# A count read ahead of the gather, overflow pieces nested in each other, and a last expert done by halves of its inner features

## The chip, the cores and the metric

The kernel runs on one core of a Trainium2 chip. The core has a matrix engine (TensorE, PE in the rows; its weight loads stand as PEld), three engines for elementwise work (VectorE or DVE, ScalarE or ACT, GpSimd or POOL), a queue engine that only issues transfers here (SyncE, SP), and 16 DMA engines that move data between the off-chip memory (HBM) and the on-chip memory (SBUF). Matrix results land in eight accumulator banks (PSUM). The metric is the device time of one execution in microseconds (us), less is better.

## What is computed

One encoder block: a token mixer (attention and a state-space scan, not touched here), then a mixture of experts over 256 tokens of 1024 features, with 32 experts of 1024 inner features, of which each token takes four.

```python
logits = xt @ w_router + b_router
top_val, top_idx = lax.top_k(logits, TOP_K)
top_w = jax.nn.softmax(top_val, axis=-1)
combine = jnp.sum(jax.nn.one_hot(top_idx, N_EXPERTS, dtype=xt.dtype) * top_w[..., None], axis=1)
for e in range(N_EXPERTS):
    gu = xt @ w_gate_up[e] + b_gate_up[e]
    gate = jnp.minimum(gu[:, :EXPERT_FF], SWIGLU_LIMIT)
    up = jnp.clip(gu[:, EXPERT_FF:], -SWIGLU_LIMIT, SWIGLU_LIMIT)
    act = (up + 1.0) * gate * jax.nn.sigmoid(SWIGLU_ALPHA * gate)
    out = out + combine[:, e:e + 1] * (act @ w_down[e] + b_down[e])
...
res = res + gate_f * _rmsnorm(ffn, p(g_post_ffn))
```

All of it is float32. The weights of one expert are 8 MiB for gate and up and 4 MiB for down.

## The kernel before

**Weights.** All weight tiles pass through one ring of SBUF slots of 1 MiB (`consumed`, L134). A load is issued on SP when a slot is released, which is when PE has read the tile that was in it. Each load also waits for the eighth load before it to have landed, since there are eight completion semaphores in turn. An expert has 12 loads: eight tiles of `w_gate_up` (128 of the 1024 input features by all 2048 columns, in rows of 8 KiB) and four of `w_down` (256 inner features by 1024 columns, in pieces of 4 KiB). The last expert's four `w_down` tiles are cut another way: 512 inner features by 512 columns, in pieces of 2 KiB, so that one half of the output columns can be finished before the other.

**Start of the experts (L995 to L1048).** Matmuls with a triangle of ones give each token its rank in each expert's list (`rank`) and each expert's count of tokens (`cnt`). `keep_warm` issues matmuls whose result nobody reads. `select` makes a 0/1 matrix for two experts, and `gather` multiplies it with the token rows, so that `xg` holds up to C = 64 tokens for each of the two experts.

**The loop (L1211 on).** The body for expert e is written out 32 times, engine by engine, in this order: `more(e, n)`, the rest of an expert with more than 64 tokens; `count(e + 1)`, which reads the next expert's count into a register of PE, ACT and DVE; `gate_up`, 64 tokens by 2048 columns, the two halves of the columns side by side in the array; `glu`; `scatter` of the expert before; half a `gather` for a later pair; `turn`, which transposes; `hint(e + 1, n)`, which tells the sequencers which way the next branch goes; `sel_T`; `down`. `down` leaves `py`, which is copied to `y` at the start of the next round.

**Overflow.** `more` is a branch over four pieces of code, for tokens 64 to 95, 96 to 159, 160 to 223 and 224 to 255. The first stands straight behind the branch. Each other piece has a branch of its own, one behind the other, so that an expert with 65 to 96 tokens comes past three further branches that all skip their piece. A piece reads all 12 tiles of its expert, and none is released until the main part that follows has read them. The profiled data have one such expert, number 11.

**Ahead of the loop** stand four matmuls with a zero tile that clear the four output banks `oacc` (L1206), then `count(0)` and `hint(0, n)`, then the branch of `more(0, n)`.

**The last expert** leaves the loop behind `glu` and `scatter`. Then come `sel_T`, `turn`, and for each half `c` of the output columns: `down` for that half alone, a copy to `y`, a `scatter` of that half, and the part of the final norm that can be done (`final`).

Of the kernel before, what the change touches and what calls it, by code (L numbers as in the profile page):

```python
# [9 lines left out]
F32 = mybir.dt.float32  # L10
# [8 lines left out]
P = 128  # L19
# [15 lines left out]
WARM = (11, 4, 4, 5)  # L35
# [39 lines left out]
def tile_hybrid_block(  # L75
# [42 lines left out]
    for e in range(NE):  # L118
        for k in range(KD):
            add_k(w_gate_up[0, e], k, 1, 0, 2 * FF)  # L120
# [10 lines left out]
    def consumed(n):  # L131
# [3 lines left out]
        while free and ring["next"] < len(loads):  # L135
# [3 lines left out]
            t3, s3, nk = t.rearrange("p (k n) -> p k n", k=shape[1]), src.rearrange("(k p) n -> p k n", p=P), shape[1]  # L139
            step = nk // 2 if i + 1 == len(loads) else nk  # L140
            for k in range(0, nk, step):
                sp.dma_start(t3[:, k:k + step], s3[:, k:k + step])
# [28 lines left out]
    ident_b = pers.tile([P, P], BF16, name="ident_b")  # L171
    wr = pers.tile([P, KD, NE], F32, name="wr")
# [7 lines left out]
    dve.memset(ones_b, 1.0)  # L180

# [816 lines left out]
    idle = pq("u", 1)  # L998
# [34 lines left out]
    sel_n = select((0, 1), 0, C)  # L1033
    for ks in HALF:
        gather(sel_n, xgs[0], ks)
# [13 lines left out]

    oacc = [[mq.tile([P, 512], F32, name=f"o{t}{hf}", tag=f"o{2 * t + hf}") for hf in range(2)] for t in range(2)]  # L1050
# [30 lines left out]
    def from_ring(e):  # L1081
        def get(k, o, w):
            i, k2 = W_MOE + 12 * e + k, k - KD
            if k >= KD and e + 1 < NE:
                i, o = W_MOE + 12 * e + KD + k2 // 2, 1024 * (k2 % 2) + o
            elif k >= KD:
                i, o = W_MOE + 12 * e + KD + 2 * (o // 512) + k2 // 4, 512 * (k2 % 4) + o % 512
            return wt[i][:, o:o + w]
# [75 lines left out]

    def more(e, n):
# [28 lines left out]
    engines = [ET.PE, ET.Activation, ET.DVE]  # L1194

    def count(e):
        return nc.values_load(cnt[0:1, e:e + 1], engines=engines, min_val=0, max_val=S)

    def hint(e, n):
        tc.mark_branch_hint_location(f"more{e}", hint=(n > C), engines=engines)  # L1200

    zero_b = mo.tile([3 * NE, P], BF16, name="zero_b")
    dve.memset(zero_b, 0.0)
    for t in range(2):
        for hf in range(2):
            pe.matmul(oacc[t][hf], zero_b, bias3[:, 0:512], start=True, stop=False, skip_group_check=True)  # L1206

    n = count(0)
    hint(0, n)
    py = None  # L1210
    for e in range(NE):  # L1211
# [3 lines left out]
        if e + 1 < NE:  # L1215
            n = count(e + 1)
# [14 lines left out]
        if e + 1 == NE:  # L1231
            break
# [21 lines left out]

    spare = [free.pop(0).tile([P, SLOT], F32, name=f"spare{i}", tag="w") for i in range(2)]
    jk = spare[1][:, 0:512]
    fo = [[spare[0][:, 1024 * t + 512 * i:1024 * t + 512 * i + 512] for i in range(2)] for t in range(2)]

    rsf = []

    def final(t, hf):
        if t is None:
            for i in range(2 * hf):
                dve.tensor_mul(fo[i][0], oacc[i][0], gbf[0])
            return
        act.activation(jk, oacc[t][hf], AF.Square, accum_out=tiny[:, 4 + 2 * t + hf:5 + 2 * t + hf])
        if hf == 0:
            return
        rsf.append(norm_of(4, t))
        if t == 0:  # L1270
            dve.tensor_mul(fo[0][1], oacc[0][1], gbf[1])
        else:
            act.activation(fo[0][1], fo[0][1], AF.Copy, scale=rsf[0])
            for t, i in ((0, 0), (0, 1), (1, 0), (1, 1)):
# [50 lines left out]
```

## Time and profile before

| | |
|---|---|
| median of three runs | 1322.29 us (1318.12 to 1325.5) |
| the profiled execution's own time | 1321.95 us |
| its span from first to last instruction | 1320.2 us |
| mean granted TensorE clock | 0.978 of 2.4 GHz |
| busy share of the span | PE 89%, DVE 27%, ACT 21%, POOL 2% |
| moved to and from HBM | 466.01 MB, mean 353 GB/s |

The busy shares are averages over stages with different limits: the token mixer up to about 320 us, the start of the experts, the expert loop from 345 us, and the end from about 1290 us. A row of the view by windows gives, for one stretch, its length, each engine's busy time with the number of instructions, the granted clock as a share of full speed (0.50 is 1.2 GHz, 1.00 is 2.4 GHz), the mean busy share of the 16 DMA engines (just over 1.00 where they are full), and what they moved. In the timeline a row has start, duration, engine, line, operation and operands, and in brackets how long the engine sat idle before it and what ended that.

### The profile page before, as it was taken

What the parts mean: (1) busy time and instruction counts of PE and PEld (TensorE: products, weight loads), DVE (VectorE), ACT (ScalarE), POOL (GpSimd) and SP (SyncE); (2) the same over time, 40 slices, a digit from 0 to 9 for tenths busy, and PEclk for the clock granted to TensorE, in tenths of its full rate; (3) what the DMA queues carried; (4) which work ended last, traced back from release to release, by engine and by line L of the source; (5) the groups of instructions that cost most, each with busy time, mean ns of one, the idle gap of its engine ahead of it and who ended that gap; (6) DMA issues with size and microseconds to landing.
All of it is one profiled execution on the core that took longest, in us unless ns stands there. A gap on an engine that the chain in (4) does not pass through costs nothing. (4 is left out here: it accounts for less than half of the span.)

```text
span 1320.2 us, 17110 instructions
## 1 busy us (share of the span) xinstructions
PE 1172.1 (89%) x6842; PEld 580.0 (44%) x6842; DVE 360.5 (27%) x763; ACT 279.1 (21%) x617; POOL 24.9 (2%) x35
## 2 busy tenths in 40 slices
PE   3799989988799999989949999999999999998986
PEld 1788867766333333333423333333333433333322
DVE  0685664457121111211111111211112111111113
ACT  1576556643110000110110001100001011000001
POOL 0100100000000000000000000000000000000000
PEclk9899999999799999999989999999999999999999
DMA  8877745477599999999988999999999999999992
GB/s 313 255 246 249 229 156 192 174 296 292 233 417 412 415 414 415 414 414 413 415 345 317 413 413 413 414 412 414 417 414 409 415 416 414 412 415 411 409 387 94
DMA packets 113469, 466.01 MB, mean 353 GB/s; under 512 B 10955, under 2 KB 34163, under 8 KB 79507
## 3 DMA queue, kind: packets, MB, share of 16 engines
q1 hardware_dynamic: 112576, 462.39, 88.6%
q8 instruction: 109, 1.79, 0.6%
q10 hardware_dynamic: 723, 1.33, 0.3%
q14 instruction: 61, 0.50, 0.1%
HBM read 462.65 MB, written 1.05 MB: 351 GB/s over the span
## 5 line engine op out<-in xcount | busy, mean ns | idle before, releaser
L1104 PE MATMUL pq_g<-w,xg 128*64 128x512 f32 x1024 | 270.9, 601 | 4.1 <-DMA w<-in_w_gate_up_dram 3.1
L1104 PE MATMUL pq_u<-w,xg 128*64 128x512 f32 x1024 | 269.2, 598 | 2.3 <-issue 2.3
L1142 PE MATMUL pq_u<-w,aT 128*64 128x512 f32 x1008 | 226.8, 595 | 2.2
L1116 ACT ACTIVATE sg<-g 128x512 f32<-128x512 f32 (+1 forms) x33 | 20.6, 623 | 730.8 <-DVE g L1115 708.8
L1115 DVE TENSOR_SCALAR g<-pq_g 128x512 f32<-128x512 f32 (+1 forms) x33 | 22.6, 684 | 481.9 <-PE pq_g L1104 266.1
L1104 PEld LDWEIGHTS pq_u<-w,xg 128*64 128x64 f32 x1024 | 75.7, 138 | 144.9 <-issue 142.8
L1104 PEld LDWEIGHTS pq_g<-w,xg 128*64 128x64 f32 x1024 | 75.1, 138 | 139.0 <-issue 117.4
L1142 PEld LDWEIGHTS pq_u<-w,aT 128*64 128x64 f32 x1008 | 70.6, 137 | 136.7 <-issue 124.7
L376 PE MATMUL ps_pj<-hh,wh 128*128 128x256 f32 x296 | 89.6, 303 | 3.6 <-DVE hh L434 3.6
L368 DVE TENSOR_TENSOR wl<-w,wh 128x1024 fp32r<-128x1024 f32 x60 | 74.7, 1246 | 59.0 <-ACT wh L367 58.9
L376 PE MATMUL ps_pj<-hh,wl 128*128 128x256 f32 x296 | 85.6, 289 | 2.4 <-DVE wl L368 2.4
L376 PE MATMUL ps_pj<-hl,wh 128*128 128x256 f32 x296 | 85.5, 289 | 0.0
L1214 DVE COPY y<-pq_u 128x512 f32<-128x512 f32 x31 | 21.4, 692 | 228.4 <-PE pq_u L1142 227.5
L1025 PEld LDWEIGHTS pq_m<-sel,xt 128*128 128x128 f32 x544 | 64.8, 195 | 24.0 <-issue 23.2
L1025 PE MATMUL pq_m<-sel,xt 128*128 128x128 f32 (+1 forms) x544 | 70.9, 285 | 0.0
L1028 ACT ACTIVATE xg<-pq_m,modT,g 128x128 f32<-128x128 f32 x128 | 48.1, 456 | 106.5 <-PE pq_m L1025 106.5
L367 ACT ACTIVATE wh<-w 128x1024 fp32r<-128x1024 f32 x60 | 63.5, 1058 | 29.0 <-PE ps_t L376 10.8
L1153 PE MATMUL o<-y,sT 64*128 64x512 f32 x256 | 65.6, 615 | 1.6 <-DVE y L1290 1.6
L376 PEld LDWEIGHTS ps_pj<-hh,wh 128*128 128x128 f32 x296 | 58.3, 197 | 9.5 <-issue 9.0
L376 PEld LDWEIGHTS ps_pj<-hh,wl 128*128 128x128 f32 x296 | 57.9, 196 | 2.9 <-DVE wl L368 2.8
L376 PEld LDWEIGHTS ps_pj<-hl,wh 128*128 128x128 f32 x296 | 58.0, 196 | 0.1
L1100 PE MATMUL pq_g<-bias,kb 96*64 96x512 bf16 (+1 forms) x68 | 13.7, 406 | 46.0 <-DVE y L1214 26.4
(301 smaller groups left out, 1001.8 us busy)
## 6 DMA issues: line engine op xcount, KB each, us to landing
w<-in_w_gate_up_dram SPq DMA_DIRECT2D x256, 1024.0 KB, 19.0
w<-in_w_down_dram SPq DMA_DIRECT2D x127, 1024.0 KB, 20.0
w<-in_w_ada_dram SPq DMA_DIRECT2D x24, 1024.0 KB, 5.2
w<-in_w_in_dram SPq DMA_DIRECT2D x22, 1024.0 KB, 13.0
w<-in_w_out_dram SPq DMA_DIRECT2D x8, 1024.0 KB, 4.8
xt<-in_x_dram ACTq DMA_DIRECT2D x1, 1024.0 KB
w<-in_w_down_dram SPq DMA_DIRECT2D x2, 512.0 KB
out_dram<-xt SPq DMA_DIRECT2D x4, 256.0 KB, 2.2
```

Source lines behind the costliest of these rows:

```text
L367: act.activation(hi.bitcast(F32R), src, AF.Copy)
L368: dve.tensor_sub(lo.bitcast(F32R), src, hi)
L376: pe.matmul(out_ap, u, v, start=first and i == 0, stop=last and i == 2, skip_group_check=True)
L1025: pe.matmul(p[:, w * i:w * i + w], res[:, t, k * 128:(k + 1) * 128], sel[:, t], start=(t == 0), stop=(t == 1))
L1028: act.activation(xg[:, k], p[:, w * i:w * i + w], AF.Identity, bias=m_shift[:, k:k + 1], scale=g1[:, 8 + k:9 + k])
L1100: pe.matmul(dst[cs * q:cs * q + cs, 0:w], kbv["e3"][0:3 * NE, e:e + 1].to_broadcast([3 * NE, cs]), bias3[:, o:o + w], start=True, stop=Fal ...
L1104: pe.matmul(dst[cs * q:cs * q + cs, 0:w], xg[:, k], weight(k, o, w), start=False, stop=(k == KD - 1), tile_position=(0, cs * q), skip_grou ...
L1115: dve.tensor_scalar(g, pg, 7.0, None, op0=OP.min)
L1116: act.activation(s, g, AF.Sigmoid, scale=1.702)
L1142: pe.matmul(py[cs * q:cs * q + cs, 0:w], a4[:, k % nj, k // nj, :], weight(KD + k, w * q, w), start=(k == 0), stop=(k == KD - 1), tile_pos ...
L1153: pe.matmul(oacc[t][hf], sT[64 * q:64 * q + 64, 128 * t:128 * t + 128], y[64 * q:64 * q + 64, :], start=False, stop=False, tile_position=( ...
L1214: dve.tensor_copy(y, py)
```

## The change

Three edits, one at each end of the loop and one inside `more`.

1. `count(0)` and `hint(0, n)` stand ahead of the first `gather`. The matmuls that clear `oacc` take the place of the nine `keep_warm` matmuls between the rank matmuls, two and two (`clear`); the zero tile is written at the kernel's start.
2. The overflow pieces are nested: the branch for a later piece stands inside the piece before it, with a hint ahead of that piece, and its skipped side leads past all later pieces at once.
3. The last expert's `w_gate_up` is loaded by halves of its inner features: four tiles hold gate and up columns of features 0 to 511 for all input features, four those of 512 to 1023, each as two transfers of 512 KiB in pieces of 2 KiB. Its `w_down` is cut as for the other experts, in pieces of 4 KiB. The computation goes by the same halves: `gate_up_half(0)`, `glu_half(0)`, the scatter before, `gate_up_half(1)` with the first half's transposes inside, `glu_half(1)`, and `down_piece` for both halves of the output columns at once. One final norm follows, on DVE and ACT alone.

```diff
@@ weight loads
+            if e + 1 < NE:
+                add_k(w_gate_up[0, e], k, 1, 0, 2 * FF)
+            else:
+                f = 512 * (k // 4)
+                loads.append(([P, 2, 2, 512], w_gate_up[0, e, 256 * (k % 4):256 * (k % 4) + 256].rearrange(
+                    "p (g n) -> p g n", g=2)[:, :, f:f + 512]))
...
-            if e + 1 < NE:
-                add_k(w_down[0, e], 2 * i, 2, 0, D)
-            else:
-                add_k(w_down[0, e], 4 * (i % 2), 4, 512 * (i // 2), 512)
+            add_k(w_down[0, e], 2 * i, 2, 0, D)
@@ start of the experts
+    def clear(t):
+        for hf in range(2):
+            pe.matmul(oacc[t][hf], zero_b[:, 0:1].to_broadcast([3 * NE, P]), bias3[:, 0:512], start=True, stop=False, skip_group_check=True)
...
-    keep_warm(idle, WARM[2])
+    clear(0)
...
-    keep_warm(idle, WARM[3])
+    clear(1)
...
     sel_n = select((0, 1), 0, C)
...
+    n = count(0)
+    hint(0, n)
     for ks in HALF:
         gather(sel_n, xgs[0], ks)
@@ overflow
+    def rest(e, n, i, chunk):
+        last = i + 1 == len(MORE)
+        if not last:
+            lo = MORE[i + 1][0]
+            tc.mark_branch_hint_location(f"more{e}_{i}", hint=(n > lo), engines=engines)
+        chunk(*MORE[i])
+        if not last:
+            with tc.If(n > lo, preferred_fallthrough_block=True, label=f"more{e}_{i}"):
+                rest(e, n, i + 1, chunk)
...
         with tc.If(n > C, preferred_fallthrough_block=True, label=f"more{e}"):
-            chunk(*MORE[0])
-            for lo, cs in MORE[1:]:
-                with tc.If(n > lo):
-                    chunk(lo, cs)
...
+            rest(e, n, 0, chunk)
@@ last expert
+    gate_up_half(0, range(KD))
+    glu_half(0)
+    scatter(C, y, sTs[(e - 1) % 2])
+    gate_up_half(1, range(4))
+    turn_half(0)
+    gate_up_half(1, range(4, KD))
+    glu_half(1)
+    py = pq("m", 2)
+    down_piece(0, (0, 1))
+    turn_half(1)
+    down_piece(0, (2, 3))
+    down_piece(1, range(4))
...
+    dve.tensor_copy(y[0:C], py[0:C])
+    act.activation(y2[C:P], py[C:P], AF.Copy)
...
+    for t in range(2):
+        for hf, y_ in enumerate((y, y2)):
+            pe.matmul(oacc[t][hf], sT[C * hf:C * hf + C, 128 * t:128 * t + 128], y_[C * hf:C * hf + C, :],
+                      start=False, stop=True, tile_position=(C * hf, 0), skip_group_check=True)
+        for hf in range(2):
+            act.activation(jk, oacc[t][hf], AF.Square, accum_out=tiny[:, 4 + 2 * t + hf:5 + 2 * t + hf])
+            dve.tensor_mul(fo[t][1 - hf], oacc[t][1 - hf], gbf[1 - hf])
+        rsf.append(norm_of(4, t))
+    for t in range(2):
+        for hf, sl in enumerate(halves):
+            dve.scalar_tensor_tensor(res[:, t, sl], fo[t][hf], rsf[t], res[:, t, sl], op0=OP.mult, op1=OP.add)
+            sp.dma_start(out_rows[128 * t:128 * t + 128, sl], res[:, t, sl])
-    for c in range(2):
-        py, rs_ = pq("gu"[c], 1), slice(64 * c, 64 * c + 64)
-        down(e, a4, C, py, (c,))
-        dve.tensor_copy(y[rs_], py[rs_])
-        final(None, c)
-        scatter(C, y, sTs[e % 2], (c,), lambda t: final(t, c))
```

On PE, at the start of the experts, the order before was this, from the first gather (L1025) over the clearing of the output banks (L1206) to the read of the first count (L1197 and L1200); the hint (L1320) and the branch of `more(0, n)` (L1188) follow directly.

```order
L1025 MATMUL pq_m<-sel,xt 128x128 x16
L1206 LDWEIGHTS zero_b
L1206 MATMUL o_3509<-bias_82,zero_b 128x512
L1206 LDWEIGHTS zero_b
L1206 MATMUL o_3510<-bias_82,zero_b 128x512
L1206 LDWEIGHTS zero_b
L1206 MATMUL o_3511<-bias_82,zero_b 128x512
L1206 LDWEIGHTS zero_b
L1206 MATMUL o_3512<-bias_82,zero_b 128x512
L1197 TENSOR_LOAD cnt
L1197 ISA x2
L1200 REGISTER_ALU
```

And this is PE's order there in the changed kernel, from the second pair of clearing matmuls (L1012) to the branch (L1223).

```order
L1012 LDWEIGHTS zero_b
L1012 MATMUL o_3452<-bias_82,zero_b 128x512
L1012 LDWEIGHTS zero_b
L1012 MATMUL o_3453<-bias_82,zero_b 128x512
L1052 TENSOR_LOAD cnt
L1052 ISA x2
L1055 REGISTER_ALU
L1381 BRANCH_PREFETCH_HINT
L1040 MATMUL pq_m<-sel,xt 128x128 x16
L1223 COMPARE_AND_BRANCH
```

The clearing and the read of the count have moved ahead of the gather's 16 matmuls, and the branch now stands straight behind the gather.

On PE, inside the overflow code of one expert before, a piece ends with its scatter (L1153) and the jumps that close it; then comes the next piece's branch, and then that piece's gather (L1025).

```order
L1153 MATMUL o_3512<-ym,sT_3513 128x512
L1191 UNCONDITIONAL_BRANCH x2
L1191 COMPARE_AND_BRANCH
L1025 MATMUL pq_m<-sel,xt 128x64 x16
L1100 LDWEIGHTS kb
```

The same place in the changed kernel:

```order
L1177 MATMUL o_3453<-ym,sT_3530 128x512
L1197 COMPARE_AND_BRANCH
L1194 REGISTER_ALU
L1381 BRANCH_PREFETCH_HINT
L1040 MATMUL pq_m<-sel,xt 128x64 x16
L1124 LDWEIGHTS kb
```

No jump closes a piece before the next branch any more; each piece begins with the hint for the branch at its own end, about 500 PE instructions later.

On SP, the last expert's loads before, from the last two of its eight tiles of `w_gate_up`:

```order
L142 DMA w_25581<-in_w_gate_up_dram 128x2048
L142 DMA w_25587<-in_w_gate_up_dram 128x2048
L142 DMA w_26203<-in_w_down_dram 128x4x512
L142 DMA w_26209<-in_w_down_dram 128x4x512
L142 DMA w_26215<-in_w_down_dram 128x4x512
L142 DMA w_26221<-in_w_down_dram 128x2x512 x2
```

And in the changed kernel:

```order
L145 DMA w_26387<-in_w_gate_up_dram 128x2x512 x2
L145 DMA w_26394<-in_w_gate_up_dram 128x2x512 x2
L150 DMA w_27038<-in_w_down_dram 128x2x1024
L150 DMA w_27044<-in_w_down_dram 128x2x1024
L150 DMA w_27050<-in_w_down_dram 128x2x1024
L150 DMA w_27056<-in_w_down_dram 128x1024 x2
```

The pieces of 512 columns (2 KiB) have moved from the four tiles of `w_down` to the eight of `w_gate_up`, and each of those eight is two transfers.

## Rows read from the trace of the kernel before

**Rows 1.** The page's DMA share in 40 slices of 33 us, and GB/s.

```profile
DMA  8877745477599999999988999999999999999992
GB/s 313 255 246 249 229 156 192 174 296 292 233 417 412 415 414 415 414 414 413 415 345 317 413 413 413 414 412 414 417 414 409 415 416 414 412 415 411 409 387 94
```

**Rows 2.** View by windows: the start, the steady loop, the stall, the last loads.

```profile
core 0: us, PE busy (x) PEld busy (x) DVE busy (x) ACT busy (x) POOL busy (x), PEclk, DMA share, GB/s
336.00:352.00 16.00, 8.56 (x24) 2.57 (x26) 2.07 (x13) 2.84 (x6) 0.00 (x0) 0.57 0.16 51
400.00:640.00 240.00, 223.53 (x1102) 85.79 (x1100) 40.31 (x85) 22.32 (x56) 0.00 (x0) 1.00 1.02 414
682.00:702.00 20.00, 7.86 (x28) 2.66 (x30) 0.00 (x0) 0.00 (x0) 0.00 (x0) 0.57 0.40 150
684.00:690.00 6.00, 0.00 (x0) 0.00 (x0) 0.00 (x0) 0.00 (x0) 0.00 (x0) 0.50 0.63 244
1280.00:1284.00 4.00, 2.91 (x16) 0.57 (x14) 0.00 (x0) 0.00 (x0) 0.00 (x0) 1.00 0.70 272
1284.00:1290.00 6.00, 5.39 (x24) 1.58 (x24) 2.10 (x4) 0.63 (x1) 0.00 (x0) 1.00 1.01 361
```

**Rows 3.** Line L1188, the branch of `more`, 369 to 600 us: duration in ns.

```profile
L1188 PEldq COMPARE_BRANCH  x9: 2960/3257/3452, 369.5 to 596.0; - x9
```

**Rows 4.** Timeline of the start: PE, and SP's first issue after it.

```profile
331.47 4.02 PE L1025 MATMUL pq_m<-sel,xt 128*128 128x128 f32 x32
338.87 1.89 PE L1206 MATMUL o<-bias,zero_b 96*128 96x512 bf16 x4 [3.38 <-DVE zero_b L1203]
345.33 0.64 PE L1100 MATMUL pq_g<-bias,kb 96*64 96x512 bf16 x2 [4.57 <-PEq L1188]
349.84 4.56 SPq L142 DMA_DIRECT2D w<-in_w_down_dram  x3
```

**Rows 5.** Lines L1188 and L1197 at the start, PE's sequencer: duration in ns, start.

```profile
L1188 PEldq COMPARE_BRANCH  x1: 3872/3872/3872, 340.5 to 340.5; - x1
L1197 PEldq TENSOR_LOAD <-cnt x1: 492/492/492, 339.4 to 339.4; - x1
```

**Rows 6.** Lines L1188 and timeline of PE about one branch of the steady loop.

```profile
L1188 PEldq COMPARE_BRANCH  x1: 3283/3283/3283, 397.7 to 397.7; - x1
395.50 6.61 PE L1142 MATMUL pq_u<-w,aT 128*64 128x512 f32 x30
403.00 0.41 PE L1100 MATMUL pq_g<-bias,kb 96*64 96x512 bf16 x2 [0.90 <-DVE y L1214]
```

**Rows 7.** Timeline behind the overflow piece: PE, and SP's last issue before it.

```profile
677.39 1.89 PE L1156 MATMUL o<-ym,sTaT 128*128 128x256 f32 x8
694.14 0.64 PE L1100 MATMUL pq_g<-bias,kb 96*64 96x512 bf16 x2 [14.86 <-issue]
671.46 31.42 SPq L142 DMA_DIRECT2D w<-in_w_down_dram  x4
```

**Rows 8.** Line L1191, branches of the further pieces; DMA queue of instructions, 677 to 694 us.

```profile
L1191 PEldq COMPARE_BRANCH  x1: 340/340/340, 677.4 to 677.4; - x1
L1191 PEldq COMPARE_BRANCH  x1: 6000/6000/6000, 679.5 to 679.5; - x1
L1191 PEldq COMPARE_BRANCH  x1: 7224/7224/7224, 685.7 to 685.7; - x1
q8 instruction: 4, 0.07, 2.3%
```

**Rows 9.** Chain that ended last, in order of time, from the last expert's loads.

```profile
1246.34 20.09 DMA w<-in_w_down_dram
...
1266.49 19.93 DMA w<-in_w_gate_up_dram
...
1292.69 7.07 PE pq_g L1142 x16
...
1302.50 7.03 PE pq_u L1142 x16
```

**Rows 10.** Line L142, one issue on SP; timeline of the end, DVE.

```profile
L142 SPq DMA_DIRECT2D w<-in_w_down_dram x1: 8352/8352/8352, 1274.0 to 1274.0; - x1
1314.62 2.33 DVE L1279 SCALAR_TENSOR_TENSOR xt<-spare,tiny,xt 128x512 f32<-128x512 f32 x2
```

More of the change, by code (lines that the diff above doesn't have):

```diff
@@ L1033, in tile_hybrid_block, with count, hint @@
     sel_n = select((0, 1), 0, C)
+    engines = [ET.PE, ET.Activation, ET.DVE]
+    def count(e):
+        return nc.values_load(cnt[0:1, e:e + 1], engines=engines, min_val=0, max_val=S)
+    def hint(e, n):
+        tc.mark_branch_hint_location(f"more{e}", hint=(n > C), engines=engines)
+    n = count(0)
+    hint(0, n)
     for ks in HALF:
@@ L1252, in tile_hybrid_block, with gate_up_half @@
             act.dma_start(bd, b_down[0])
+    sT = sTs[e % 2]
+    sel_T(e, 0, C, [sT])
+    xg, weight = xgs[e // 2 % 2][:, :, C:2 * C], from_ring(e)
+    pg, pu = pq("g", 1), pq("u", 1)
+    u, g, s = [mo.tile([P, 512], F32, name=n_, tag=n_) for n_ in ("u", "g", "sg")]
+    aT = mo.tile([P, 512], F32, name="aT", tag="aT")
+    def gate_up_half(f, ks):
+        cols = slice(256 * f, 256 * f + 256)
+        for k in ks:
+            for dst, off in ((pg, 0), (pu, FF)):
+                os = [(q, slice(C * q, C * q + C), off + 512 * f + 256 * q) for q in range(2)]
+                if k == 0:
+                    for q, rows_, o in os:
+                        pe.matmul(dst[rows_, cols], kbv["e3"][0:3 * NE, e:e + 1].to_broadcast([3 * NE, C]),
+                                  bias3[:, o:o + 256], start=True, stop=False, tile_position=(0, C * q), skip_group_check=True)
+                for q, rows_, o in os:
+                    pe.matmul(dst[rows_, cols], xg[:, k], weight(k, o, 256), start=False, stop=(k == KD - 1),
+                              tile_position=(0, C * q), skip_group_check=True)
+            if k % 2:
+                consumed(W_MOE + 12 * e + 4 * f + k // 2 + 1)
@@ new lines, in glu_half, with turn_half @@
+    def glu_half(f):
+        h = slice(256 * f, 256 * f + 256)
+        dve.tensor_scalar(g[:, h], pg[:, h], 7.0, None, op0=OP.min)
+        act.activation(s[:, h], g[:, h], AF.Sigmoid, scale=1.702)
+        dve.tensor_scalar(u[:, h], pu[:, h], 7.0, -7.0, op0=OP.min, op1=OP.max)
+        dve.scalar_tensor_tensor(u[:, h], u[:, h], 1.0, g[:, h], op0=OP.add, op1=OP.mult)
+        dve.tensor_mul(u[:, h], u[:, h], s[:, h])
+    def turn_half(f):
+        p = pq("m", 2)
+        for j in range(2):
+            o = 256 * f + 128 * j
+            pe.transpose(p[:, 128 * j:128 * j + 128], u[:, o:o + 128], ident)
+        for j in range(2):
+            o = 256 * f + 128 * j
+            if j:
+                dve.tensor_copy(aT[:, o:o + 128], p[:, 128:256])
+            else:
+                act.activation(aT[:, o:o + 128], p[:, 0:128], AF.Copy)
@@ new lines, in down_piece @@
+    def down_piece(f, ks):
+        for k in (4 * f + k_ for k_ in ks):
+            o = 256 * f + 128 * (k % 2) + C * (k % 4 // 2)
+            for q in range(2):
+                pe.matmul(py[C * q:C * q + C, :], aT[:, o:o + C], weight(KD + k, 512 * q, 512),
+                          start=(k == 0), stop=(k == KD - 1), tile_position=(0, C * q), skip_group_check=True)
+    gate_up_half(0, range(KD))
[3 more added lines that the diff above has]
+    turn_half(0)
```

73 lines of the change are left out of this document (22 added, 51 removed).

## The prediction

> **What bounds the kernel now.** I read the page's DMA line first. From the eleventh slice on (345 us) the transfers run at about 414 GB/s with two exceptions, a dip in slices 20 and 21 and a hole ahead of it all [rows 1]. The view by windows says the same of the steady loop: in 240 us the DMA share is 1.02 and 414 GB/s are moved [rows 2]. An expert's 12 MiB (12.58 MB) take 12.58/0.414 = 30.4 us of that. PE's busy time there is 223.5 of 240 us, but it is not the bound: nine branches of the loop lie between 369.5 and 596.0 us, eight rounds of 28.3 us [rows 3]. PE's round is shorter than the transfers' and PE runs up against the loads in the end. So in the loop only one thing costs time: microseconds in which the DMA engines stand idle because no slot comes free. There are two such holes. From 336 to 352 us the share is 0.16, so 16 × 0.84 = 13.4 us are idle; from 682 to 702 us it is 0.40, so 20 × 0.60 = 12.0 us are idle [rows 2]. The third place is the end: the chain that ended last goes from the last expert's loads of `w_down` and `w_gate_up` (the last landing at 1286.42) through the two halves of `down` on PE to the output [rows 9].
>
> **A, the start.** PE's gather (32 matmuls) ends at 335.49. Then PE waits 3.38 us for DVE's zero tile, clears for 1.89 us, waits 4.57 us for its sequencer, and starts the first expert at 345.33; SP issues its next load at 349.84 [rows 4]. Inside the 4.57 us are the read of the count, 0.492 us, and the branch, 3.872 us [rows 5]. The change takes the clearing and its wait out of this stretch, and puts the read of the count ahead of the gather. The sequencer then comes to the branch while the gather's last matmuls are still queued. How far ahead, a branch in the steady loop shows: it starts at 397.7, the matmuls before it end at 395.50 + 6.61 = 402.11 (a group with gaps), and it takes 3.28 us, so it is over 1.1 us before the queue runs dry; the next expert's first matmul comes at 403.00, 0.90 us after the one before [rows 6]. At the start the queue holds less, since a gather's matmuls are short: 4.02/32 = 0.126 us each. I estimate 2 us of cover, half of the steady loop's 4.4. The gather itself starts later, by the read of the count with its semaphores and the hint: 0.5 us for the read, 0.8 taken. So: gather ends 336.3, branch from 334.3 to 338.0 (3.3 to 3.9 us), and 0.85 to 0.9 us from its end to the first matmul [rows 6] gives 338.8 instead of 345.33, 6.5 us earlier.
>
> What of it the DMA gets: with PE's start 6.5 us earlier the first slots come free 6.5 us earlier, if the clock stays as it was (0.57 over the stretch, that is mostly the lower level, 1.2 GHz [rows 2]). PE stood idle for 3.38 us before; now it stands for about 2.5. If the clock stays at 2.4 GHz the first matmuls run in half the time and about 2 us more are had. Bounds: 2.5 (the read makes PE stop ahead of the gather, the clock falls there, and the gather's 4.02 us become 8) and 9. I take 7.0, near the lower of the two regular cases. The nine `keep_warm` matmuls that go stood in a stretch where PE waits for other engines anyway; I cost them at nothing, and if their absence cools the clock that is the 2.5.
>
> **B, the overflow.** One expert has 65 to 96 tokens. Its piece's scatter ends at 679.28, and PE's next matmul is at 694.14, 14.86 us later; SP's four loads there spread from 671.46 over 31.42 us, right across the hole [rows 7]. In this gap PE's sequencer goes through three skips: 0.34 us at 677.4, 6.00 us at 679.5, 7.22 us at 685.7 [rows 8]. The clock is at 1.2 GHz in the middle of the hole [rows 2]. Nested, the first of the three jumps past everything, and the other two do not happen. Its jump is now far and its hint lies some 500 PE instructions back. The price lies between a hinted jump of the steady loop, 2.96 to 3.45 us [rows 3], and the unhinted 7.22. It starts at 677.4 as before, about 1.9 us ahead of PE's end of queue, so PE resumes at 677.4 + 3.3 + 0.9 = 681.6, or at 685.5. I take the first, since a hint is given, and the nine hinted branches of [rows 3] all lie near it. PE starts 12.5 us earlier or 8.6, and so do the loads that it frees. The hole's idle time is 12.0 us; it does not go quite to nothing, since a restart at the lower clock frees its first slots late (4.5 us from PE's first matmul to SP's next issue at the start [rows 4]): I leave 2 us of it. So 10.0; bounds 8.4 (the jump at 7.2) and 11.3 (the clock stays at 2.4 GHz). The hint instructions themselves cost below 0.1 us and stand in code that one expert runs. ACT and DVE pass the same branches; they wait for PE there.
>
> **C, the last expert.** Its order turns from "all of gate and up, then the rest" to halves, so PE has work left for less time after the last load. Price: its 8.39 MB come in pieces of 2 KiB. Before, only its `w_down` did: from 1284 to 1290, the DMA share was 1.01 and 361 GB/s were moved, where 8 and 4 KiB pieces move 414 [rows 2]. I estimate 8.39/0.361 = 23.2 us for gate and up instead of 20 (the last landing 1266.42 + 20.0 = 1286.42 [rows 9]); so 1266.4 + 23.2 = 1289.6, and `w_down` with 4.19 MB at 414 GB/s takes 10.1: the last load lands at 1299.8. Behind it PE has the last two pairs, 4 × 0.22 = 0.9 us: `py` is complete at 1300.8 (0.1 for the semaphore). PE's own chain is hardly longer: the 32 matmuls of `down`, now with both output halves side by side, take 6.61/30 = 0.22 us each as in the loop [rows 6], 7.05 in all, where each half alone took 7.07 before [rows 9]; from 1289.6 with an estimated 2.4 us for the last gate-up tile, the turns and what of GLU nothing covers, 1299. Before, the second half of `down` ended at 1302.50 + 7.03 = 1309.53 [rows 9]. That is 8.7 us earlier. Behind it the final norm was split over engines and started with the first half; now everything comes after `py`: one more square and multiply of 512 columns for each token tile on ACT and DVE, and a DVE instruction of the last kind takes 1.16 us (2.33/2 [rows 10]), partly side by side. I estimate 1.3 to 1.7 us more. Net 7.0; bounds 3 (the pieces and PE's chain both worse) and 10.
>
> **Sum.** The changes act on three separate stretches, and idle DMA time saved in A and B reaches the end whole, because from there on loads run without a gap and PE's round is shorter [rows 2, 3]: 7 + 10 + 7 = 24. The profiled execution took 1321.95 us, the median of the runs is 1322.29, so it is a typical one: 1321.95 − 24 = **1298 us**.
>
> [...] Unhinted jumps cost 6.0 and 7.2 us, and in 677 to 694 us the instruction queue q8 moved four packets [rows 8]. [...]
>
> **Rivals.**
> 1. The hint of the nested piece is lost, because it is some 500 instructions old when its branch comes; the jump takes 7.2 us as the unhinted ones do [rows 8]. Against it: hints of the loop are given several us ahead and hold [rows 3]. B is 8.4 or less, and with the cold clock behind it the time is 1300. Chance 0.15.
> 2. SP becomes the bound of the last expert. One load cut in 2 KiB pieces held SP for 8.35 us [rows 10], and around it, from 1280 to 1284, the DMA share was 0.70 [rows 2]. If such dips spread over the 23 us, C loses 4: 1302. Against it: the dip is short, and the loads are now two transfers of half the size. Chance 0.12.
> 3. A fails: PE stops for the count ahead of the gather, the clock falls to 1.2 GHz and the branch still waits, so A is 2.5: 1303. Speaking for it: the clock is low all through this stretch now [rows 2]. Chance 0.08.
> 4. Pieces of 2 KiB cost nothing, the 361 GB/s being an effect of the end of the ring: C is 10.8, the time 1294. Against it: the share is full in that row [rows 2]. Chance 0.05. [...]
> 5. Slower than before: the nested code makes the jump of every expert's outer branch longer than its cover. It now takes about 3.3 us with 4.4 us of cover [rows 6]. At the unhinted 6.0 to 7.2 [rows 8] 1.6 to 2.8 us show in each round, and if the clock falls too, about 2 us more. From 338.8 to 1289.6 there are 950.8 us for 31 rounds and one overflow piece, which I put at a round: 950.8/32 = 29.7. Up to there, 1.4 us above the 28.3 of [rows 3], PE stays hidden behind the loads; the whole gain is eaten at 29.7 + 24/32 = 30.45, 2.15 us above. With 1.6 + 2 the round is 31.9, 2.2 over the 29.7, and the time 1298 + 32 × 2.2 = 1368. Against it: the code jumped over is the same code, and its hint stays where it was. Chance 0.03.
>
> **How the numbers follow.** The forecast has 0.55 and gives 1296 to 1301 by the spreads of A (6.5 to 8.6), B (9 to 11) and C (5.5 to 8). Rivals 1 and 4 lie in or beside it, 2 and 3 at 1302 and 1303; two of them together, or one with a piece of the other, reach 1306; the two best bounds of A and C give 1290 to 1292. So 1290 to 1306 holds what the named cases but the last make likely; 0.02 is left for what is not named. A change of 0.5% (6.6 us) is about what a measurement of this kernel can tell. To be no faster than that, A, B and C would have to give less than 6.6 together, for which two of the three must fail whole, or rival 5 must hold: faster 0.92, same 0.04, slower 0.04.
>
> **What would show it.** A: PE's first L1124 matmul (the first of an expert, L1100 before) near 338.8 and a DMA share over 0.5 in 336 to 352. Wrong if the branch of `more(0)` lies behind the gather's end. B: one jump of about 3.3 us on PE's sequencer behind the overflow piece, and no gap of over 4 us; at 7 us rival 1 holds. C: the last gate-up landing 23 us after the last load of expert 30, 361 GB/s at a full share, `py` within 1.5 us of the last load; a share below 0.9 there is rival 2. The outer branches at 2.96 to 3.45 us, else rival 5. The prediction is wrong as a whole if the holes close and the end does not move: then PE's round, not the DMA, bounds the loop.

## The result and the profile after

The changed kernel takes 1302.05 us (median of four runs, 1301.95 to 1304.92), the kernel before 1322.18 beside it; the ratio is 0.9859, 95% interval 0.983 to 0.9888. That is 20.1 us less where 24 were forecast (the ratio is not the quotient of the two medians, which is 0.9848). The profiled execution took 1302.06 us, with a span of 1300.0.

The page's GB/s in 40 slices of 32.5 us, of the changed kernel:

```profile
GB/s 312 259 250 258 207 184 178 157 315 263 268 415 414 412 415 412 416 413 415 415 405 406 413 415 413 414 414 414 415 415 404 415 410 415 404 413 408 416 345 205
```

The dip to 345 and 317 GB/s in the middle of [rows 1] is gone, the one at the start is not. At the other end the last slice but one shows 345, where the last expert's loads with small pieces stand. The view by windows says how much of each is left:

```profile
core 0: us, PE busy (x) PEld busy (x) DVE busy (x) ACT busy (x) POOL busy (x), PEclk, DMA share, GB/s
330.00:332.00 2.00, 0.97 (x4) 0.15 (x3) 1.40 (x8) 0.00 (x0) 0.00 (x0) 0.57 0.99 410
332.00:337.00 5.00, 4.72 (x22) 4.75 (x23) 0.04 (x1) 0.94 (x3) 0.00 (x0) 0.50 1.00 412
336.00:352.00 16.00, 12.40 (x55) 5.42 (x55) 2.00 (x12) 4.83 (x11) 0.00 (x0) 0.75 0.37 132
...
682.00:702.00 20.00, 19.06 (x98) 7.83 (x96) 3.70 (x7) 2.79 (x7) 0.00 (x0) 1.00 1.00 399
...
1240.00:1260.00 20.00, 16.38 (x84) 5.90 (x82) 4.91 (x10) 1.78 (x4) 0.00 (x0) 1.00 0.92 322
...
1260.00:1272.00 12.00, 11.71 (x100) 6.39 (x94) 1.64 (x4) 0.42 (x1) 0.00 (x0) 1.00 1.03 376
...
1280.00:1282.00 2.00, 2.00 (x7) 0.33 (x3) 0.00 (x0) 0.00 (x0) 0.00 (x0) 0.50 0.54 211
```

In the hole at the overflow the share went from 0.40 [rows 2] to 1.00: 12.0 us idle before, none now (0.6 in the wider stretch from 672 to 702, where it was 11.7). At the start it went from 0.16 to 0.37, that is 16 × 0.63 = 10.1 us idle where 13.4 were: 3.3 us won. The clock stood at 0.50 through most of the gather (332 to 337 us). PE's timeline at the three places:

```profile
332.28 6.11 PE L1040 MATMUL pq_m<-sel,xt 128*128 128x128 f32 x32 [1.21 <-DVE top L1066]
341.98 0.64 PE L1124 MATMUL pq_g<-bias,kb 96*64 96x512 bf16 x2 [3.60 <-DVEq L1223]
...
679.31 0.41 PE L1124 MATMUL pq_g<-bias,kb 96*64 96x512 bf16 x2 [1.15 <-issue]
...
1276.10 0.65 PE L1287 MATMUL pq_g<-w,xg 128*64 128x256 f32 x4 [0.26 <-DMA w<-in_w_gate_up_dram]
1276.58 0.60 PE L1287 MATMUL pq_u<-w,xg 128*64 128x256 f32 x4
1278.75 3.30 PE L1316 MATMUL pq_m<-w,aT 128*64 128x512 f32 x8 [1.57 <-DMA w<-in_w_down_dram]
1281.98 0.69 PE L1304 MATMUL pq_m<-kc,u 128*128 128x128 f32 x2
1282.60 5.37 PE L1316 MATMUL pq_m<-w,aT 128*64 128x512 f32 x24
```

The gather took 6.11 us, not 4.02 [rows 4], and the first expert starts at 341.98, 3.35 us sooner than before and 3.2 us later than predicted. Behind the overflow PE now stands 1.15 us instead of 14.86 [rows 7]. At the end `py` is complete at 1287.97; in [rows 9] it was 1309.53. PE does not run through there: it stands 1.57 us for the first load of `w_down`, and behind that the clock is 0.50 and eight matmuls of `down` take 3.30 us (1.89 without such a wait, with the last expert alone below). The branches on the sequencers (L1223 is the outer branch of an expert, L1197 that inside the overflow code):

```profile
L1223 PEldq COMPARE_BRANCH  x1: 3127/3127/3127, 335.4 to 335.4; - x1
...
L1223 DVEq EVENT_SEMAPHORE  x1: 21/21/21, 341.9 to 341.9; - x1
...
L1223 PEldq COMPARE_BRANCH  x10: 2942/3174/3697, 365.9 to 621.2; - x10
...
L1197 PEldq COMPARE_BRANCH  x2: 197/276/354, 676.2 to 678.4; - x2
```

PE's own first branch is over at 338.5. What PE's first matmul waited for is DVE, which passes the same branch at 341.9, since the combine weights stand ahead of it in DVE's queue and their exponentials stand behind the gather's copies on ACT. The outer branches of the loop cost what they did [rows 3]. The jump over the later overflow pieces costs 0.35 us.

SP's first load after the start is issued at 346.50, 3.3 us sooner than in [rows 4]. The first load of the last expert's gate and up is issued at 1236.13:

```profile
346.50 0.38 SPq L150 DMA_DIRECT2D w<-in_w_down_dram  x1
...
1236.13 29.87 SPq L145 DMA_DIRECT2D w<-in_w_gate_up_dram  x16
```

Load by load, SP's issues in the changed kernel stand 3.0 us earlier ahead of the overflow (633.24 against 636.26 for the same load; 0.3 of it was there before the gather), and 12.7 earlier near the end of the loop (1200.05 against 1212.72). So the start gave 2.7 us and the overflow 9.7. The last expert and the final norm gave 7.5: with the 0.3 from ahead of the gather 20.2 in all, the difference of the spans.

### The profile page after: what moved, and what is told of

Read it like the earlier page. It is cut to its first block, busy times and chain, and to the rows that moved or that the text cites. A ratio compares the mean times of both kernels' runs of the same rounds, so it can differ in the third digit from the quotient of the medians.

```text
span 1300.0 us, 17236 instructions
## 1 busy us (share of the span) xinstructions
PE 1166.8 (90%) x6901; PEld 586.7 (45%) x6901; DVE 360.4 (28%) x768; ACT 279.8 (22%) x619; POOL 23.7 (2%) x34
## 5 line engine op out<-in xcount | busy, mean ns | idle before, releaser
L1128 PE MATMUL pq_g<-w,xg 128*64 128x512 f32 x992 | 263.2, 598 | 2.8 <-DMA w<-in_w_gate_up_dram 2.8
L1128 PE MATMUL pq_u<-w,xg 128*64 128x512 f32 x992 | 263.2, 596 | 1.3 <-issue 1.3
L1166 PE MATMUL pq_u<-w,aT 128*64 128x512 f32 x992 | 219.7, 595 | 2.1
L1177 PE MATMUL o<-y,sT 64*128 64x512 f32 x248 | 61.6, 615 | 0.0
L1095 PE MATMUL pq_m<-kc,selw 128*128 128x128 f32 x66 | 16.3, 315 | 29.0 <-DVE selw L1091 28.2
```

The source lines that it names most:

```text
L1095: pe.transpose(p[:, 128 * t:128 * t + 128], selw[:, t].rearrange("p d c -> p (d c)"), ident)
L1128: pe.matmul(dst[cs * q:cs * q + cs, 0:w], xg[:, k], weight(k, o, w), start=False, stop=(k == KD - 1), tile_position=(0, cs * q), skip_grou ...
L1166: pe.matmul(py[cs * q:cs * q + cs, 0:w], a4[:, k % nj, k // nj, :], weight(KD + k, w * q, w), start=(k == 0), stop=(k == KD - 1), tile_pos ...
L1177: pe.matmul(oacc[t][hf], sT[64 * q:64 * q + 64, 128 * t:128 * t + 128], y[64 * q:64 * q + 64, :], start=False, stop=False, tile_position=( ...
```

## The experiments

**Each part alone.** The three parts of the diff, one at a time, on the kernel before. Of each the core lines stand here.

```diff
@@ start alone
+    clear(0)
+    clear(1)
+    n = count(0)
+    hint(0, n)
@@ overflow alone
+            rest(e, n, 0, chunk)
@@ last expert alone
+    gate_up_half(0, range(KD))
...
+    down_piece(1, range(4))
```

> The kernel before with the edit at the start of the experts alone. Theory: the start is worth the 3 us by which SP's loads stood earlier in the changed kernel ahead of the overflow, because PE waits there for DVE's branch behind the combine weights: PE's first expert matmul near 342.0, loads 3.0 us earlier, time 1319. Rival: the start is worth the predicted 7 us, and the two other edits give back 4: time 1315.

> The kernel before with the nested overflow pieces alone. Theory: the two skips of 6.0 and 7.2 us go, and no other jump becomes dear; PE's gap of 14.86 us falls to about 1.2, the DMA's idle time there from 12.0 to about 1 us, time 1311.5 (10 to 11 us less). Rival: the gain needs the earlier start, since without it the ring is emptier at the overflow; then under 8 us, time over 1314.

> The kernel before with the last expert's halves alone. Theory: from the last gate and up matmul to py 10.8 us instead of 21.1, the loads with 2 KiB pieces about 1.4 us later, the final norm 1.3 us longer, so 7.5 us less: time 1314.5. Rival: the pieces of 2 KiB cost the 3 us that were predicted and the gain at py is 11: then gate and up land 23 us after the last load of the expert before, time 1315 to 1316.

| | median us | runs | ratio | 95% interval |
|---|---|---|---|---|
| start alone | 1314.35 | 1311.18 to 1319.95 | 0.9949 | 0.9931 to 0.9967 |
| overflow alone | 1313.55 | 1311.0 to 1314.78 | 0.9935 | 0.9917 to 0.9952 |
| last expert alone | 1314.97 | 1313.65 to 1316.17 | 0.9945 | 0.9929 to 0.9962 |

Beside a median of 1322.93 for the kernel before these are 8.6, 9.4 and 8.0 us by the medians, 25.9 in all, where together they gave 20.1. By the ratios they are 6.7, 8.6 and 7.3, 22.6 in all, against 18.6 for the changed kernel as first timed and 21.2 as timed again (below). The intervals reach 2 to 4 us either way, so the times alone do not tell whether the parts add up. The start alone gave more than the 3 us that I expected from the changed kernel's trace, and the rival's 7 us is nearer. The windows and rows of that run, and one window of the kernel before, show two reasons:

```profile
336.00:352.00 16.00, 12.42 (x60) 5.09 (x60) 2.00 (x12) 4.81 (x11) 0.00 (x0) 0.89 0.60 205
672.00:702.00 30.00, 17.05 (x74) 6.41 (x74) 0.00 (x0) 0.00 (x0) 0.00 (x0) 0.77 0.72 279
...
333.92 3.81 PE L1032 MATMUL pq_m<-sel,xt 128*128 128x128 f32 x32 [1.63 <-DMA w<-in_w_gate_up_dram]
...
686.90 0.64 PE L1115 MATMUL pq_g<-bias,kb 96*64 96x512 bf16 x2 [12.95 <-issue]
...
L1206 PEldq COMPARE_BRANCH  x1: 4132/4132/4132, 674.1 to 674.1; - x1
```

```profile
672.00:702.00 30.00, 13.74 (x78) 6.79 (x72) 1.63 (x4) 2.17 (x8) 0.00 (x0) 0.72 0.61 239
```

At the start 6.4 us are idle, 7.0 less than before: here the clock is 0.89 and the gather took 3.81 us, with the same instructions that took 6.11 in the changed kernel. And at the overflow 8.4 us are idle (30 × 0.28) where 11.7 were (30 × 0.39). These 3.3 us can't be won twice, since the nested pieces take the hole whole. But they are not all the work of the earlier start: PE stands there 12.95 us instead of 14.86, because one skip took 4.13 us in this run where it took 6.00 [rows 8]. That is 1.9 of the 3.3; that the rest comes from the earlier start is not shown. The last expert alone shows the end without a wait for any load:

```profile
1293.05 0.60 PE L1280 MATMUL pq_u<-w,xg 128*64 128x256 f32 x4
1293.48 1.89 PE L1309 MATMUL pq_m<-w,aT 128*64 128x512 f32 x8
1295.30 0.44 PE L1297 MATMUL pq_m<-kc,u 128*128 128x128 f32 x2
1295.66 5.37 PE L1309 MATMUL pq_m<-w,aT 128*64 128x512 f32 x24
```

No row has an idle time in brackets: PE's own work sets the end there, and `py` is complete at 1301.03 (1300.8 predicted), 7.4 us behind the last matmul of gate and up (1293.05 + 0.60). In the changed kernel, with the wait and the lower clock, these are 10.8 us (1277.18 to 1287.97).

**The combine weights ahead of the gather.**

```diff
     hint(0, n)
+    comb = mo.tile([P, 2, NE], F32, name="comb")
...
     for ks in HALF:
         gather(sel_n, xgs[0], ks)
-    comb = mo.tile([P, 2, NE], F32, name="comb")
...
```

> The changed kernel with the combine weights computed ahead of the gather (ACT's and DVE's instructions for them moved). Theory: PE's first expert matmul waits for DVE's branch, which stands behind the combine weights; moved, PE starts when its own branch and the read of the next count are over, near 339.5 instead of 342.0, and the time falls by 2.4 us to 1299.6. Rival: PE's own branch, 3.2 us, is what counts, or the copies of the gather on ACT are; then PE starts at 341 or later and the time stays within 1 us of 1302.

1299.71 us (1298.09 to 1301.65), ratio 0.9829 (0.981 to 0.9848): the time that the theory named, but not for its reason. PE's timeline, and its and DVE's rows of the branch:

```profile
334.80 3.81 PE L1040 MATMUL pq_m<-sel,xt 128*128 128x128 f32 x32 [1.54 <-DMA w<-in_w_gate_up_dram]
342.35 0.41 PE L1124 MATMUL pq_g<-bias,kb 96*64 96x512 bf16 x2 [3.74 <-PEq L1223]
```

```profile
L1223 PEldq COMPARE_BRANCH  x1: 4970/4970/4970, 336.5 to 336.5; - x1
L1223 DVEq EVENT_SEMAPHORE  x1: 21/21/21, 336.8 to 336.8; - x1
```

DVE is through at 336.8, and PE still stands 3.74 us behind the gather: now its own branch, 4.97 us this time, comes last; it ends at 341.43, 0.92 us ahead of PE's first matmul. The wait on DVE (3.60 us in the changed kernel) hid a second one of nearly the same length. The theory that DVE alone held the start falls.

**No hints inside the overflow code.**

```diff
     def rest(e, n, i, chunk):
-            tc.mark_branch_hint_location(f"more{e}_{i}", hint=(n > lo), engines=engines)
```

> The changed kernel without the hints inside the overflow pieces. Theory: the hint, given 26 us ahead of its branch, is what makes the far jump cost 0.35 us; without it the jump takes 6 to 7.2 us as the unhinted skips of before did, PE's gap grows from 1.2 to about 8 us, and the DMA loses some 5 us: 1307. Rival: one far jump at the end of a piece is cheap with or without a hint, since the first skip of before took 0.34 us without one; then the gap stays at 1.2 us and the time at 1302.

1302.13 us (1297.78 to 1305.89), ratio 0.9843 (0.9813 to 0.9873). Both were wrong in part. The jump, PE's gap and the DMA:

```profile
L1196 PEldq COMPARE_BRANCH  x2: 197/3080/5962, 672.3 to 678.6; - x2
```

```profile
679.52 0.64 PE L1124 MATMUL pq_g<-bias,kb 96*64 96x512 bf16 x2 [5.27 <-issue]
```

```profile
672.00:702.00 30.00, 23.85 (x109) 10.14 (x107) 3.70 (x7) 2.69 (x8) 0.00 (x0) 0.89 0.93 372
```

Without a hint the far jump costs 5.96 us, so the hint is what makes it 0.35. But a PE that stands 5.27 us leaves only 30 × 0.07 = 2.1 us of the DMA idle there (0.6 in the changed kernel, with a share of 0.98), because loads already issued cover most of it: SP issues one at 668.23, and its next at 684.04. The time does not show it, in four runs that spread over 8 us. The 5.96 us are near the 6.00 of the first long skip without a hint before [rows 8]; what the sequencer waits for in such a jump is not shown.

**The loop's hint straight behind the count.**

```diff
         n = count(e + 1)
+        hint(e + 1, n)
...
-        hint(e + 1, n)
         sel_T(e, 0, C, [sTs[e % 2]])
```

> The changed kernel with the hint for each expert's branch straight behind the read of its count, some 25 us ahead of the branch instead of 5.9. Theory: a branch ends no sooner than 7 to 9 us after its hint (5.9 + 3.2 in the loop, 3.7 + 3.1 and 2.2 + 4.6 at the start), so with 25 us it takes 0.1 to 0.5 us, as the nested one did; the time does not move (within 1 us of 1302), since the branch was covered. Rival: 3 us is what a taken branch of the loop costs with any hint; then it stays at 2.9 to 3.7 us.

1299.54 us (1297.4 to 1301.8), ratio 0.9824 (0.9805 to 0.9843). PE's branches of the loop:

```profile
L1223 PEldq COMPARE_BRANCH  x31: 89/367/3752, 365.5 to 1252.0; - x31
```

The median fell from 3.17 to 0.37 us, as the theory has it. But ten of the 31 still take 3.0 to 3.8 us with the same 23 us of notice. That a branch merely ends 7 to 9 us after its hint is therefore not the whole rule, and what sets those ten apart stays open. It is not chance alone: seven of the ten (experts 2, 7, 12, 17, 25, 27 and 30) are long again in the trace of the three edits together, further down. Whether the 2.5 us in the medians come from the hints is unclear too: the intervals of the two ratios overlap, and PE's round in the loop stayed at 28.3 us.

**The nine matmuls back.**

```diff
-WARM = (11, 4)
+WARM = (11, 4, 4, 5)
+    idle = pq("u", 1)
+    keep_warm(idle, WARM[2])
     clear(0)
...
+    keep_warm(idle, WARM[3])
     clear(1)
```

> The changed kernel with the nine matmuls back that keep PE busy between the rank matmuls. Theory: in the profiled run of the changed kernel the granted clock fell ahead of the gather because these were gone, and the gather took 6.1 instead of 4.0 us; with them it takes 4.0 and the first expert starts 1.5 to 2 us sooner, 1300.5. Rival: the clock's fall there is a matter of the run, since with the same order and without those matmuls the gather took 3.8 us in the kernel with the start alone; then no change beyond 0.5 us.

1299.81 us (1299.38 to 1300.56), ratio 0.9824 (0.9807 to 0.984).

```profile
334.54 3.81 PE L1043 MATMUL pq_m<-sel,xt 128*128 128x128 f32 x32 [0.89 <-DMA w<-in_w_gate_up_dram]
341.94 0.41 PE L1127 MATMUL pq_g<-bias,kb 96*64 96x512 bf16 x2 [3.59 <-DVEq L1226]
```

The gather is warm, 3.81 us, and behind it the same 3.6 us pass.

**The changed kernel again, unaltered.**

> The changed kernel once more, unaltered. Theory: whether the clock falls ahead of the gather is a matter of the run, so that the kernel has two times some 3 us apart, 1302 with a cold gather of 6.1 us (as profiled) and 1299 with a warm one of 3.8 us; its median lies between, 1299 to 1302. Rival: it belongs to the kernel, always 1302, and the experiments at 1299.5 gained by their edits.

1302.62 us (1297.97 to 1304.8), ratio 0.984 (0.9819 to 0.9862).

```profile
334.91 3.81 PE L1040 MATMUL pq_m<-sel,xt 128*128 128x128 f32 x32 [1.54 <-DVE top L1066]
342.54 0.41 PE L1124 MATMUL pq_g<-bias,kb 96*64 96x512 bf16 x2 [3.82 <-DVEq L1223]
```

```profile
334.00:339.00 5.00, 3.81 (x32) 3.65 (x32) 0.34 (x2) 1.75 (x5) 0.00 (x0) 1.00 1.00 417
...
336.00:352.00 16.00, 12.18 (x65) 5.80 (x65) 2.00 (x12) 4.83 (x11) 0.00 (x0) 0.89 0.54 194
```

The same program now has a warm gather, at a clock of 1.00. So whether the clock falls ahead of it is a matter of the run, as the theory said, and the nine matmuls are not needed for a warm one. Of the eight profiled runs with this start and without the nine, six had a warm gather (a clock of 0.96 from 330 to 370 us) and two a cold one (0.83; the other, of 6.16 us, is that of the next experiment); the three with the nine were warm (0.89 from 336 to 352 us in each, as in this run). The idle time at the start is 7.4 us (16 × 0.46), 6.0 less than before. The other half of the theory falls: the span is 1300.0 again, because the mixer ended 2.6 us later in this run (the gather starts at 334.91, not 332.28) and took the gain. The windows of the mixer, of this run and of the one first profiled, show where the clock was low instead:

```profile
0.00:330.00 330.00, 283.66 (x2392) 234.17 (x2392) 191.77 (x396) 177.76 (x360) 19.67 (x30) 0.96 0.68 237
```

```profile
0.00:330.00 330.00, 282.20 (x2403) 231.23 (x2404) 193.84 (x410) 177.77 (x360) 20.26 (x31) 0.98 0.69 240
```

The warm gather goes with a colder mixer, 0.96 instead of 0.98, and so in all profiles with the new start: 0.96 where the gather is warm, 0.97 and 0.98 where it is cold. That this alone made the mixer 2.6 us longer is not shown. Also, DVE, which the row names, was not what held PE behind the gather here. It had passed at 342.26, 0.28 us ahead of PE's first matmul, where in the run first profiled it was 0.05; PE's own branch took 5.05 us and ended at 341.62, 0.92 us ahead of it, as in the run with the combine weights first. Two times 3 us apart were not seen; the five runs spread over 7 us.

**`w_down` ahead of the last half of gate and up.**

```diff
+            if e + 1 == NE and k == 3:
+                for i in range(2):
+                    add_k(w_down[0, e], 2 * i, 2, 0, D)
...
-    gate_up_half(1, range(4))
+    gate_up_half(1, range(2))
     turn_half(0)
+    gate_up_half(1, range(2, 4))
+    py = pq("m", 2)
+    down_piece(0, (0, 1))
     gate_up_half(1, range(4, KD))
```

> The changed kernel with the last expert's first two tiles of w_down loaded ahead of the second half of gate and up, and half of the first half's down done between the matmuls of that half. Theory: behind the last load PE, not the DMA, sets the end (9.2 us from the start of down to py); with 16 of the 32 matmuls of down gone from there and the last w_down tiles landing last, py is complete 4 to 6 us sooner: 1297. Rival: the last load sets the end after all, which stays at about the same time; then under 1.5 us.

1304.13 us (1302.15 to 1304.97), ratio 0.9854 (0.9837 to 0.987): nothing gained.

```profile
1273.31 1.07 PE L1292 MATMUL pq_g<-w,xg 128*64 128x256 f32 x4 [3.26 <-DMA w<-in_w_gate_up_dram]
...
1286.92 3.65 PE L1321 MATMUL pq_m<-w,aT 128*64 128x512 f32 x16 [0.37 <-ACT aT L1315]
```

The wait has moved, not gone. PE no longer stands 1.57 us ahead of `down`; it stands 3.26 us in the middle of gate and up, where it had work before, for a load that now comes behind those of `w_down`, and the matmuls behind that wait are slow again (1.07 us for four, 0.60 otherwise). Counted from the issue of the expert's first load (1237.46, and 1236.13 in the changed kernel), `py` is complete after 53.1 us instead of 51.8. My theory was wrong in looking only behind the last load.

**Gate and up of the last expert whole again.** Loads in rows of 8 KiB, all columns at once; `w_down`, `down` over both column halves and the one final norm as changed.

```diff
-    gate_up_half(0, range(KD))
...
-    down_piece(1, range(4))
+    a4 = turn(u, C, (lambda: pq("u", 1), lambda: pq("g", 1)))
+    py = pq("u", 1)
+    down(e, a4, C, py, range(2))
```

> The changed kernel, but the last expert's gate and up loaded in rows of 8 KiB and computed whole as in the other experts, with w_down, the one down for both column halves and the one final norm as changed. Theory: the gain of the last expert comes from down using both halves of the array once (7.05 us instead of twice 7.07 with a scatter between), not from the halves of the inner features, whose cover for GLU is paid for by the slower loads: gate and up end 18.8 us after the expert before, py 11.4 us later, time within 1.5 us of the changed kernel. Rival: the halves hide GLU and the transposes, 3 to 4 us, and without them the time is 1304 to 1306.

1301.0 us (1299.57 to 1302.19), ratio 0.9829 (0.9815 to 0.9844), no slower than the changed kernel.

```profile
1235.38 18.01 SPq L139 DMA_DIRECT2D w<-in_w_gate_up_dram  x8
...
1274.14 1.08 PE L1114 MATMUL pq_g<-w,xg 128*64 128x512 f32 x4 [0.54 <-DMA w<-in_w_gate_up_dram]
1275.05 1.03 PE L1114 MATMUL pq_u<-w,xg 128*64 128x512 f32 x4
...
1280.11 7.09 PE L1152 MATMUL pq_u<-w,aT 128*64 128x512 f32 x32 [0.31 <-ACT aT L1144]
```

```profile
1246.00:1266.00 20.00, 17.04 (x78) 5.10 (x74) 2.60 (x6) 0.77 (x2) 0.00 (x0) 1.00 1.01 414
```

The loads run at 414 GB/s, where the changed kernel made 322 as its pieces of 2 KiB set in (1240 to 1260) and 376 further on (1260 to 1272). Gate and up end at 1276.08 instead of 1277.18, and `py` is complete at 1287.20 instead of 1287.97; 0.8 us of that is the loop, which was further ahead in this run. Counted from the issue of the expert's first load, 1235.38 here and 1236.13 there, `py` is complete after 51.8 us in both. So the halves of the inner features gain nothing here: what they cover (GLU and the transposes) is what their slower loads and the wait behind them cost. The gain of this part is that `down` runs once with both column halves side by side, 7.09 us, instead of 7.07 and 7.03 one behind the other with a copy and a scatter between [rows 9].

**Put together.** Three edits to the start and the loop at once (nine matmuls, combine weights first, early loop hint), and then the same with the last expert whole.

```diff
+WARM = (11, 4, 4, 5)
+    keep_warm(idle, WARM[2])
+    keep_warm(idle, WARM[3])
...
     hint(0, n)
+    comb = mo.tile([P, 2, NE], F32, name="comb")
...
         n = count(e + 1)
+        hint(e + 1, n)
```

> The changed kernel with three edits to the start and the loop together: the nine matmuls back, the combine weights ahead of the gather, and each loop hint straight behind its count. Theory: with a warm gather and DVE through early, PE starts when its own first branch ends, 1 us sooner than with the nine matmuls alone: 1298.5. Rival: the start is held by the length of that first branch, 3.7 to 5.2 us, which none of the three touches: 1299.5 to 1300.5.

> The three edits to the start and the loop together with the last expert's gate and up whole. Theory: the two ends are independent, the start's 4 us and the end's 1 us add up: 1297. Rival: without the halves the earlier loop finds the last gate and up loads as late as before, and nothing is added: 1298 to 1299.

1298.06 us (1297.76 to 1299.61), ratio 0.9812 (0.9798 to 0.9825), and 1297.71 us (1295.05 to 1298.43), ratio 0.9811 (0.9795 to 0.9828). The first beats the changed kernel as first timed, 0.9859 (0.983 to 0.9888); beside its second timing (0.9819 to 0.9862) the intervals still touch. Adding the whole last expert changes nothing that can be told. In the first, PE's start looks as before, with the branch last again:

```profile
334.22 3.81 PE L1043 MATMUL pq_m<-sel,xt 128*128 128x128 f32 x32 [0.77 <-DMA w<-in_w_gate_up_dram]
341.67 0.41 PE L1127 MATMUL pq_g<-bias,kb 96*64 96x512 bf16 x2 [3.64 <-PEq L1226]
```

## Why the prediction came out as it did

The direction and the range were right, and so was the mechanism in the main: both holes shrank and the end came closer. The sum was 4 us too large, and the term that was off is A. B and C came out at their sizes, but in part by luck, since prices inside both were wrong.

**A, 7.0 predicted, 2.7 in the profiled run.** The step "gather ends 336.3" assumed the gather's 4.02 us at a clock of 1.00; it started where predicted (332.28 against 331.47 + 0.8) but ran at a clock of 0.50 for the most part and ended at 338.39, 2.1 us later. Then "0.85 to 0.9 us from its end to the first matmul" of a branch that ends at 338.0 gave a gap of 2.5 us; the five runs shown have 3.6 to 3.8. The 0.9 holds where PE's own branch comes last (0.92 in the second trace of the changed kernel), though the row that I took it from, [rows 6], shows another wait, for DVE's copy of `y`. I costed PE's branch and left out that DVE has to pass it too, behind the combine weights; and PE's branch itself took 3.1 to 5.2 us there, where I had put 3.3 to 3.9. Taking DVE out of the way showed the branch right behind it. Where the gather was warm, the idle time at the start fell by 6.0 and 7.0 us, close to the forecast; load by load, counted from the mixer's end, the start gave 4.9 us (the changed kernel again) and 5.8 (the start alone), and up to half of that had been lost in a later mixer. So the profiled run showed the larger part of the third rival (a cold gather, 2.5 us), to which I had given 0.08; it depends on the run.

**Sum over separate stretches.** The step that the three terms add up is neither refuted nor confirmed: the parts alone sum to 22.6 us by their ratios, the changed kernel has 18.6 and 21.2, and the intervals are as wide as the difference. The trace of the start alone shows one overlap: 3.3 us of its gain lay in the hole at the overflow, which the nested pieces close anyway. Of these 1.9 are a skip that was shorter in that run; the rest is open.

**B, 10.0 predicted, 9.7 measured,** 9.4 alone. The size was right, its working was not. The jump cost 0.35 us, not 3.3: I priced a hint given 26 us ahead by hints given 5.9 us ahead. And the price hardly matters: with 5.96 us the idle time grew by 1.5 us (2.1 against 0.6), near the 1.6 that the bound of 8.4 for a jump at 7.2 had put on it, and the time showed no difference. The first rival would have cost nothing that can be told. I also left 2 us of the hole open; 0.6 were.

**C, 7.0 predicted, 7.5 measured,** 8.0 alone. `py` came 8.9 us earlier than the loop's gain explains (1309.53 − 12.7 − 1287.97), against 8.7; the final norm took 12.0 us from `py` to the end of the span instead of 10.7, the 1.3 predicted. The working was off in three places. I had the last load land 0.8 us behind PE's own chain (1299.8 against 1299); with the last expert alone PE's own work sets the end, and in the changed kernel it is the first load of `w_down` that PE waits for, 1.57 us, not the last. The pieces of 2 KiB ran slower than the 361 GB/s predicted at first, 322 at a share of 0.92, which is the second rival in part, and faster after, 376 at a full share; over all of gate and up they cost less than the 3.2 us that I took (23.2 against 20): PE has the last tile 40.0 us after the expert's first load was issued (1236.13 to 1276.10), with rows of 8 KiB after 38.8 (1235.38 to 1274.14). And the halves of the inner features, which I took for the edit's point, are not where the gain is.

**Rival 5** (a longer outer branch) did not come: 2.94 to 3.70 us, against 2.96 to 3.45 before. **Rival 4** (free pieces of 2 KiB) is not borne out: 376 GB/s at a full share, where rows of 8 KiB make 414, and 1.2 us later on PE.

## What to carry to other kernels

When a wait is removed from one engine at a join of branches, look at when each of the other engines passes the same branch: the next wait may be of the same length (here 3.74 us where it had been 3.60). Time savings both alone and together, and before calling a difference of the sums an overlap compare it with the intervals and look in the trace for what one run had by chance, here a skip shorter by 1.9 us. A warm stretch in one profile can go with a colder one ahead of it (here a gather at 1.00 behind a mixer at 0.96 instead of 0.98): compare the whole way up to it. At the end of a load-bound loop look at every wait of the last round before moving a load ahead; the wait can move with it (here from 1.57 us ahead of `down` to 3.26 in the middle of gate and up).

## What the runs showed of the hardware

What a jump cost on PE's sequencer, by how far ahead its hint stood: 0.35 us with 26.6 us of notice, mostly 0.37 (but 3.0 to 3.8 in ten of 31) with 23, 2.9 to 3.7 with 5.9 in the first ten rounds, 3.1 and 3.5 with 3.7, 3.7 to 5.2 with 2.2 to 2.4, and 5.96 without; without one, two jumps one behind the other took 6.00 and 7.22 before [rows 8], 4.13 and 7.25 with the start alone. With its hint 0.1 us ahead the first branch took 3.87 us [rows 5], within the 3.7 to 5.2 of 2.2 to 2.4 us.

The same instructions of the gather ran mostly at a clock of 0.50 in one run (6.11 us) and at 1.00 in another of the same kernel (3.81 us). In the first the clock fell from 330 to 332 us (a mean of 0.57), while PE did four short matmuls, 0.97 us in all, and waited for DVE; in the second it was 1.00 from 330 to 339, and its mean over the mixer ahead of that 0.96 instead of 0.98. The kernel's own work up to that place was the same in both.

Sixteen transfers of 512 KiB in pieces of 2 KiB moved 322 GB/s at a share of 0.92 from 1240 to 1260 us, in part beside loads in pieces of 4 KiB, and 376 at a full share from 1260 to 1272, where rows of 8 KiB move 414. They held SP for a median of 0.72 us each and up to 4.30, but the longest is not theirs alone: with gate and up whole the same expert's first load, in rows of 8 KiB, held it 4.29.
